# A hybrid encoder layer with 32 experts: the last two products trade places, the overflow count is read early, the final norm's row and the bias rows move

## The chip, the cores and the metric

The kernel runs on 1 core of one Trainium2 chip. The metric is the device time of one execution in microseconds; smaller is better. A core has a TensorE (PE in the rows; its weight loads are PEld), a VectorE (DVE), a ScalarE (ACT), a GpSimd (POOL), and a SyncE (SP) that here does nothing but issue transfers and read a few registers. Sixteen DMA engines carry the transfers.

## The reference

One encoder layer over 256 tokens of width 1024, and a final norm. A mixer (gated delta rule beside a short convolution) is followed by a mixture of experts, and the change lies in the second of these alone.

```python
def moe_ffn(h, router_w, router_b, w1, b1, w2, b2):
    logits = (hf @ router_w + router_b).astype(jnp.float32)
    top_val, top_idx = lax.top_k(logits, TOP_K)          # 4 of 32 experts for each token
    gates = jax.nn.softmax(top_val, axis=-1)
    ...
    def expert_block(args):
        gu = x_blk @ w1[e] + b1[e]                       # 1024 -> 2048
        gate, up = jnp.split(gu, 2, axis=-1)
        gate = jnp.minimum(gate, SWIGLU_LIMIT)
        up = jnp.clip(up, -SWIGLU_LIMIT, SWIGLU_LIMIT)
        act = gate * jax.nn.sigmoid(SWIGLU_ALPHA * gate) * (up + 1.0)
        return act @ w2[e] + b2[e]                       # 1024 -> 1024
    ...
x = x + gt_f * moe_ffn(...)
return rmsnorm(x, final_norm_w)
```

All 32 experts are used, in float32: 8 MB of `w1` and 4 MB of `w2` each.

## The kernel before, in words

After the mixer, the 32 experts are worked in 16 pairs, p = 0 to 15; two pairs form one of eight groups q (`NQ`). Pairs 0 and 1 are the experts 0 to 3; from group 1 on the experts are sorted by their load, and SP reads their numbers into registers (`pidx_i`, L1576) to form the addresses.

**First product, w1(p)** (`w1_pair`, L1372). Eight steps k. Each loads two tiles of 1 MB, one for each expert (`w1_load`), and makes 16 matmuls into four PSUM banks `pss[0..3]`: for each bank c, four matmuls j side by side on 32 columns of the array each (L1380). The fourth step calls `mid()`. After the last step four small matmuls add the bias (`w1_bias`, L119). Then `swiglu` (L1359 to L1363) makes half 0 from the banks 0 and 2, half 1 from 1 and 3: on DVE a minimum g, a clip u and two products, on ACT a tanh. `to_ff` transposes both halves on PE (L1397, eight transposes) and copies them to `aT` on ACT (L1398).

**Second product, w2(p)** (`w2_pair`, L1417). Four steps c, each again two tiles of 1 MB (L1426) and 16 matmuls (L1432). Then `combine`: DVE scales by the residual gate (L1414), PE spreads the rows back to the tokens (L1405), DVE adds to `x1` (L1407).

**Order of the pairs.** w1(0), then for p = 1 to 15: w1(p), w2(p-1), `to_ff` of p. So the swiglu of a pair has the second product of the pair before it to hide behind. Pair 15 ends with `w2_cols`: its second product in three parts of 512, 256 and 256 columns (`PARTS`; loads L1449, matmuls L1456), each followed by `combine` and by its share of the final norm (`finish_part`, L1558, L1549).

**Buffers and queues.** All weight tiles come from a ring of 18 places (`w_half`, L954): a load waits until the matmuls that read the tile 18 places before it are done. All loads go out on SP, in order, and at most eight are under way at once. A library places the instructions of each engine: it may move those that are not pinned (`pin`) past others, so the order of an engine is not always that of the program text.

**Three small things.** `final_row`, called from `mid()` of pair 2, loads the final norm's weights as two rows of 512 (L1563) and spreads them over the partitions by a matmul (L1566). Its tile `row` shares the buffer `u` of the swiglu, of which there is one. `route_rest` makes, beside the sorted order, the integer `nov`, the number of tokens that find no place in their expert's block. Behind the last `combine` every engine reads `nov` into a register (L1602) and branches (L1603): the overflow code is skipped when it is zero, as it is here.

Of the kernel before, what the change touches and what calls it, by code (L numbers as in the profile page):

```python
# [10 lines left out]
FT = mybir.dt.float32  # L11
# [3 lines left out]
AF = mybir.ActivationFunctionType  # L15
# [6 lines left out]
KT = D // 128  # L22
H = 8
NE = 32
# [4 lines left out]
NQ = 8  # L29
# [24 lines left out]
def encoder_block(ctx, tc, x, c, ada_w, ada_b, norm1_w, w_in, conv_qkv_w, a_log, dt_bias, onorm_w,  # L54
                  w_up_a, conv_sc_w, w_out_sc, w_o, norm2_w, router_w, router_b, moe_w1, moe_b1,
                  moe_w2, moe_b2, final_norm_w, out, dbg=None):
    nc = tc.nc
    V, A, G, PE = nc.vector, nc.scalar, nc.gpsimd, nc.tensor
# [22 lines left out]
    half_m = consts.tile([128, 1], FT, name="half_m")  # L81
    G.memset(half_m, -0.5)

    pin = tc.keep_in_program_order
# [25 lines left out]
    def misc(n=512):  # L110
        return pm.tile([128, n], FT, name="misc", tag="pt", bufs=2)

    def acc():
        return pm.tile([128, 512], FT, name="acc", tag=next(accs), bufs=3)

    def w1_bias(pa, bsel, b1c, pss, parts=(0, 1, 2, 3), first=False, pinned=False):
        for c in parts:
            b = 32 * c
            i = PE.matmul(pss[c], bsel[b:b + 32, pa * 128:(pa + 1) * 128], b1c[b:b + 32], start=first, stop=not first,  # L119
                          tile_position=(b, 0), skip_group_check=True)  # L120
            if pinned:
                tc.keep_in_program_order(i)
# [9 lines left out]
    with ExitStack() as mix:  # L132
# [26 lines left out]
        warm = consts.tile([128, 1], FT, name="warm")  # L159
# [6 lines left out]
        for i, b in enumerate(eb):  # L166
# [10 lines left out]
                        None, op0=OP.mult)  # L177
# [173 lines left out]
        for j in range(4):  # L351
# [12 lines left out]
            w = ep.tile([128, KT, 256], FT, name="raw", tag="raw", bufs=6) \  # L364
# [13 lines left out]
            for kk in range(2):  # L378
                k = 2 * j + kk
# [594 lines left out]
        def w1_load(p, k, regs):  # L974
            w = pre.pop((p, k), []) if p < 2 else []
            for m in range(len(w), 2):
                w.append(quarters(w1_tile(p, k, m, regs)[0]))
            return w
# [190 lines left out]
        pss0, bias_parts = [], []  # L1169
# [26 lines left out]
    work = ctx.enter_context(tc.tile_pool(name="work", bufs=1))  # L1196
# [30 lines left out]
    b1c, bsel0 = rbox[3:5]  # L1227
# [5 lines left out]
    nov = moe.tile([1, NE + 1], I32, name="nov")  # L1233
# [11 lines left out]
    def members(q):  # L1245
        off = 0
        for m, g in enumerate(GROUPS[min(q, 1)]):
            yield 4 * q + m, off, 32 * g
            off += 32 * g

    def bias_rows(q):
        bsel = work.tile([128, QS], FT, name="bsel", tag="bsel", bufs=1)
        for cpos, off, n in members(q):
            V.tensor_copy(bsel[:, off:off + n], perm[:, cpos:cpos + 1].to_broadcast([128, n]))
        return bsel
# [25 lines left out]
    for k, m, ts in ((KT - 2, 0, [fw, spare("pg"), spare("pgT")]), (KT - 2, 1, [spare("aT", 1024), spare("aT", 1024)]),  # L1281
                     (KT - 1, 0, [spare("g"), spare("g"), spare("u"), spare("th")]),
                     (KT - 1, 1, [spare("ysb"), spare("ysb"), e4])):
        c, qs = 0, []
# [40 lines left out]
    def xq_tile():  # L1325
        return work.tile([128, KT, QS], FT, name="XT", tag="XT", bufs=1)
# [11 lines left out]
    def gates_of(q):  # L1338
        pg = work.tile([128, 2, QS], FT, name="pg", tag="pg", bufs=1)
        for t in range(2):  # L1340
            for cpos, off, n in members(q):
                V.tensor_scalar(pg[:, t, off:off + n], iota[:, 0:n], rks[:, 0, t, cpos:cpos + 1],
                                rks[:, 1, t, cpos:cpos + 1], op0=OP.is_equal, op1=OP.mult)
        p = misc()
        for pa in range(2):
            for t in range(2):
                PE.transpose(p[:, (pa * 2 + t) * 128:(pa * 2 + t + 1) * 128], pg[:, t, pa * 128:(pa + 1) * 128], ident)
        gt = work.tile([128, 2, 2, 128], FT, name="pgT", tag="pgT", bufs=1)
        A.copy(gt, p.rearrange("p (a t n) -> p a t n", a=2, t=2))
        return gt  # L1350

    def owners(q):
        return [m for m, g in enumerate(GROUPS[min(q, 1)]) for _ in range(g)]
# [18 lines left out]
    def w1_pair(p, xq, bsel, pss, regs, mid):  # L1372
        q, pa = divmod(p, 2)
        own = owners(q)[4 * pa:4 * pa + 4]
        first = p == 0
        for k in range(KT):
            w = w1_load(p, k, regs)
            for c in range(4):
                for j in range(4):
                    PE.matmul(pss[c][j * 32:(j + 1) * 32], xq[:, k, (4 * pa + j) * 32:(4 * pa + j + 1) * 32],  # L1380
                              w[own[j] % 2][c], start=k == 0 and not first, stop=k == KT - 1 and first,
                              tile_position=(0, 32 * j), skip_group_check=True)
            if first and k < KT - 2:
                gather_part(P0, xq, (k + 2,))
            if k == 3:
                mid()
        if not first:
            w1_bias(pa, bsel, b1c, pss)
        return [swiglu(128, pss[half], pss[2 + half]) for half in range(2)]

    def to_ff(gs):
        aT = work.tile([128, KT, 128], FT, name="aT", tag="aT", bufs=2)
        for half in range(2):
            ps = misc()
            for i in range(4):
                c0 = 256 * (i // 2) + i % 2
                PE.transpose(ps[:, i * 128:(i + 1) * 128], gs[half][:, c0:c0 + 255:2], ident)  # L1397
            A.activation(aT[:, 4 * half:4 * half + 4], ps.rearrange("p (f n) -> p f n", f=4), AF.Copy, scale=0.5)  # L1398
        return aT
# [9 lines left out]
    def w2_rows(p, m, regs):  # L1409
        return moe_w2[0, 2 * p + m:2 * p + m + 1] if p < 2 else moe_w2[0, ds(regs[2 * (p % 2) + m], 1)]  # L1410
# [7 lines left out]
    def w2_pair(p, aT, gt, regs):  # L1418
        q, pa = divmod(p, 2)
        own = owners(q)[4 * pa:4 * pa + 4]  # L1420
        ys = [acc() for _ in range(2)]
        for c in range(4):
            w = []
            for m in range(2):
                t = w_half()
                nc.sync.dma_start(t, w2_rows(p, m, regs)[:, 256 * c:256 * c + 256].rearrange("e (p i) n -> p (e i n)", i=2))  # L1426
                w.append(t.rearrange("p (i n) -> p i n", i=2))
            for i in range(2):
                f = 2 * c + i
                for h in range(2):  # L1430
                    for j in range(4):
                        PE.matmul(ys[h][j * 32:(j + 1) * 32], aT[:, f, j * 32:(j + 1) * 32],  # L1432
                                  w[own[j] % 2][:, i, 512 * h:512 * h + 512], start=f == 0, stop=f == KT - 1,
                                  tile_position=(0, 32 * j), skip_group_check=True)
        for h in range(2):
            combine([gt[:, pa]], [scaled(ys[h], 512 * h, 512)], 512 * h, 512)
# [98 lines left out]
    xq = xq_tile()  # L1535
# [22 lines left out]
            V.tensor_tensor(xf[:, t, cs], x1[:, t, cs], fw[:, cs], op=OP.mult)  # L1558

    def final_row():  # L1560
        for h in range(2):
            row = work.tile([128, 512], FT, name="row", tag="u", bufs=1)[0:1]
            nc.sync.dma_start(row, bass.AP(tensor=final_norm_w.tensor, offset=final_norm_w.offset + 512 * h,  # L1563
                                           ap=[[D, 1], [1, 512]]))
            p = misc()
            PE.matmul(p, one_f[0:1], row, start=True, stop=True)  # L1566
            A.copy(fw[:, 512 * h:512 * h + 512], p)


    aTs, gts, regs, bsel = {}, {}, [None] * NQ, bsel0  # L1570
    nxt = []
    NP = 2 * NQ
    for p in range(NP):
        q, pa = divmod(p, 2)
        if pa == 0 and q:
            _, regs[q] = nc.values_load_multi_w_load_instructions(  # L1576
                pidx_i[0:1, 4 * q:4 * q + 4], engines=[mybir.EngineType.SP], min_val=0, max_val=NE - 1)

        def mid():
            if p == 2:  # L1580
                final_row()
            if pa == 1:
                gts[q] = gates_of(q)
                if q + 1 < NQ:
                    nxt.append(slots_of(q + 1))

        gs = w1_pair(p, xq, bsel, [acc() for _ in range(4)] if p else pss0, regs[q], mid)
        if p == 0:
            route_rest()
        if pa == 1 and q + 1 < NQ:  # L1590
            xq = gather(nxt.pop())
            bsel = bias_rows(q + 1)
        if p:
            w2_pair(p - 1, aTs.pop(p - 1), gts[(p - 1) // 2], regs[(p - 1) // 2])
        aTs[p] = to_ff(gs)
    xf = work.tile([128, KT, QS], FT, name="XT", tag="XT", bufs=1).rearrange("p (t a) b -> p t (a b)", t=2)
    for i, (c0, n) in enumerate(PARTS):
        w2_cols(NP - 1, c0, n, aTs[NP - 1], gts[NQ - 1], regs[NQ - 1])
        if i < len(PARTS) - 1:
            finish_part(xf, i)  # L1600

    n_over = nc.values_load(nov[0:1, NE:NE + 1], min_val=0, max_val=8 * NE)  # L1602
    with tc.If(n_over > 0):  # L1603
        ov = work.tile([128, KT, 128], FT, name="over", tag="aT", bufs=2).rearrange("p b n -> p (b n)")
        V.tensor_tensor(rks[:, 0], rks[:, 0], capr[:, None, :].to_broadcast([128, 2, NE]), op=OP.subtract)
        with tc.For_i(0, NE, 1) as cp:
# [6 lines left out]
            with tc.For_i(0, nb, 1) as b:  # L1613
# [7 lines left out]
                p = misc()  # L1621
# [10 lines left out]
                p = misc()  # L1632
# [4 lines left out]
                for half in range(2):  # L1637
                    pss = [acc() for _ in range(2)]
                    for gu in range(2):
                        bs = slice(32 * (2 * gu + half), 32 * (2 * gu + half) + 32)  # L1640
                        PE.matmul(pss[gu][0:32], ohe[bs].to_broadcast([NE, 32]), b1c[bs],
                                  start=True, stop=False, tile_position=(bs.start, 0), skip_group_check=True)
# [67 lines left out]
```

## Time and profile before

| what | value |
|---|---|
| median of 3 runs | 1381.16 us (1380.38 to 1382.26) |
| the profiled execution: its own time | 1382.46 us |
| the profiled execution: span of the core | 1380.7 us |
| busy share of the span: PE, DVE, ACT, POOL | 97%, 37%, 20%, 11% |
| bytes read from HBM | 486.82 MB |
| mean granted TensorE clock | 0.991 of full speed |

The profiled execution took 1.3 us longer than the median. Its span runs from the first to the last instruction. A busy PE is not PE at its peak, since matmuls are pipelined and their ends are modelled.

### The profile page before, as it was taken

Reading aid. Unit: us, or ns where it says so; the run is one execution under the profiler, and the core shown is the slowest. Engines: PE = TensorE matmul, PEld = TensorE weight load, DVE = VectorE, ACT = ScalarE, POOL = GpSimd, SP = SyncE. Lnnn points to the kernel's source line nnn. Section 1 sums busy time; section 2 is a strip of 40 time slices with the busy share of each in tenths; the row PEclk is TensorE's granted clock in tenths of the full one; section 3 lists DMA queues with packets and bytes.
Section 4 is the critical chain, followed back from the end, with each engine's and each line's share of the span. In section 5 each row is a group of like instructions: output and inputs, shape, how many; then the busy total and the mean of one; then the engine's idle time right before and its main releaser. Section 6 shows DMA issues by size and latency. Waiting matters only on the chain.

```text
span 1380.7 us, 24523 instructions
## 1 busy us (share of the span) xinstructions
PE 1338.9 (97%) x10250; PEld 688.6 (50%) x10251; DVE 512.0 (37%) x1017; ACT 280.0 (20%) x544; POOL 150.9 (11%) x125
## 2 busy tenths in 40 slices
PE   6999998899999999999999999999999999999996
PEld 4898887899996333233333333333333333333322
DVE  3377879965773332113113022120311212031123
ACT  3465562554642010000000000000000000010001
POOL 4555685000100000000000000000000000000000
PEclk9999999999999999999999999999999999999998
DMA  9978977247698999999999999999999999999995
GB/s 336 291 250 267 303 234 245 76 147 251 227 363 301 385 381 421 410 420 420 420 422 420 421 421 420 421 420 422 420 421 420 421 422 420 421 420 421 421 382 169
DMA packets 134708, 492.68 MB, mean 357 GB/s; under 512 B 11070, under 2 KB 68799, under 8 KB 86977
## 3 DMA queue, kind: packets, MB, share of 16 engines
q1 hardware_dynamic: 130548, 486.08, 89.6%
q10 hardware_dynamic: 4045, 4.98, 1.1%
q8 instruction: 82, 1.34, 0.4%
q14 instruction: 33, 0.27, 0.1%
HBM read 486.82 MB, written 4.21 MB: 356 GB/s over the span
## 4 chain that ended last, share of the span: by engine, by line
issue 65%; POOLq 0%; ACT 0%
POOLq L1705 0%; ACT XT L1678 0%
## 5 line engine op out<-in xcount | busy, mean ns | idle before, releaser
L1380 PE MATMUL acc<-wst,XT 128*32 128x512 f32 x4088 | 543.7, 595 | 0.0
L1380 PEld LDWEIGHTS acc<-wst,XT 128*32 128x32 f32 x4088 | 154.5, 110 | 350.0 <-issue 332.9
L1432 PE MATMUL acc<-wst,aT 128*32 128x512 f32 x1920 | 234.9, 595 | 2.0 <-DMA wst<-in_moe_w_dram 2.0
L1359 DVE TENSOR_SCALAR g<-acc 128x512 f32<-128x512 f32 x32 | 20.7, 687 | 387.6 <-PE acc L119 383.5
L313 PE MATMUL mm<-hh,wl 128*128 128x256 f32 (+1 forms) x520 | 149.3, 287 | 5.0 <-DVE wl L263 3.6
L311 PE MATMUL mm<-hh,wh 128*128 128x256 f32 (+1 forms) x520 | 151.3, 291 | 1.2 <-DVE cacc L556 1.2
L312 PE MATMUL mm<-hl,wh 128*128 128x256 f32 (+1 forms) x520 | 149.5, 288 | 0.0
L1432 PEld LDWEIGHTS acc<-wst,aT 128*32 128x32 f32 x1920 | 68.4, 109 | 145.6 <-issue 131.2
L88 POOL TENSOR_TENSOR rs<-ss,half_m 128x2 f32<-128x2 f32 x3 | 2.1, 703 | 1008.5 <-DVE ss L1672 943.5
L262 ACT CAST wh<-raw 128x1024 fp32r<-128x1024 f32 (+1 forms) x89 | 91.7, 1038 | 94.7 <-PE mm L312 55.0
L311 PEld LDWEIGHTS mm<-hh,wh 128*128 128x128 f32 (+1 forms) x520 | 100.2, 193 | 12.5 <-issue 8.1
L313 PEld LDWEIGHTS mm<-hh,wl 128*128 128x128 f32 (+1 forms) x520 | 100.1, 193 | 7.2 <-DVE wl L263 3.8
L312 PEld LDWEIGHTS mm<-hl,wh 128*128 128x128 f32 (+1 forms) x520 | 100.2, 193 | 0.9 <-issue 0.8
L1398 ACT ACTIVATE aT<-misc 128x512 f32<-128x512 f32 x32 | 17.6, 595 | 387.9 <-PE misc L1397 387.9
L263 POOL TENSOR_TENSOR wl<-raw,wh 128x1024 fp32r<-128x1024 f32 x36 | 87.7, 2444 | 71.6 <-ACT wh L262 65.7
L1407 DVE TENSOR_TENSOR x<-x,misc 128x512 f32<-128x512 f32 (+1 forms) x66 | 44.3, 671 | 80.1 <-PE misc L1405 80.1
L263 DVE TENSOR_TENSOR wl<-raw,wh 128x1024 fp32r<-128x1024 f32 (+1 forms) x53 | 63.8, 1209 | 24.7 <-ACT wh L262 24.3
L1360 ACT ACTIVATE th<-g 128x512 f32<-128x512 f32 x32 | 20.2, 630 | 254.6 <-DVE g L1359 210.2
L1414 DVE TENSOR_TENSOR ysb<-acc,gtf 128x512 f32<-128x512 f32 (+1 forms) x33 | 22.3, 675 | 125.6 <-PE acc L1432 113.5
L1405 PE MATMUL misc<-ysb,pgT 128*128 128x512 f32 (+1 forms) x132 | 63.9, 606 | 2.0 <-DVE ysb L1414 1.9
L1323 ACT ACTIVATE XT<-misc,mod,afc 128x256 f32<-128x256 f32 x32 | 17.3, 561 | 167.9 <-PE acc L1380 126.1
L556 DVE SCALAR_TENSOR_TENSOR cacc<-mm,col,cacc 128x254 f32<-128x254 f32 (+1 forms) x96 | 46.1, 480 | 9.0 <-ACT cacc L553 6.9
(388 smaller groups left out, 1396.9 us busy)
## 6 DMA issues: line engine op xcount, KB each, us to landing
wst<-in_moe_w_dram SPq DMA_DIRECT2D x372, 1024.0 KB, 19.8
raw<-in_w_in_dram SPq DMA_DIRECT2D x36, 1024.0 KB, 7.4
raw<-in_ada_w_dram SPq DMA_DIRECT2D x24, 1024.0 KB, 8.5
wst<-in_moe_w_dram SPq DMA_DIRECT2D x24, 256.0 KB, 7.6
wst<-in_moe_w_dram SPq DMA_DIRECT2D x11, 512.0 KB, 15.1
raw<-in_w_out_sc_dram SPq DMA_DIRECT2D x4, 1024.0 KB
raw<-in_w_up_a_dram SPq DMA_DIRECT2D x4, 1024.0 KB, 5.2
raw<-in_w_o_dram SPq DMA_DIRECT2D x4, 1024.0 KB, 13.3
```

Source lines behind the costliest of these rows:

```text
L262: a = A.copy(wh, src)
L263: b = (V if job.lo == "v" else G).tensor_tensor(wl, src, wh.bitcast(FT), op=OP.subtract)
L311: PE.matmul(ps, wh[:, k, :], ah[:, k, :], start=k == 0, stop=False, skip_group_check=True)
L312: PE.matmul(ps, wh[:, k, :], al[:, k, :], start=False, stop=False, skip_group_check=True)
L313: PE.matmul(ps, wl[:, k, :], ah[:, k, :], start=False, stop=k == KT - 1, skip_group_check=True)
L556: V.scalar_tensor_tensor(a[:, o0:o1], p[:, s0:s1], cw(j), a[:, o0:o1], op0=OP.mult, op1=OP.add)
L1359: V.tensor_scalar(g[:n], g_ps[:n], 7.0, None, op0=OP.min)
L1380: PE.matmul(pss[c][j * 32:(j + 1) * 32], xq[:, k, (4 * pa + j) * 32:(4 * pa + j + 1) * 32], w[own[j] % 2][c], start=k == 0 and not first, ...
L1405: PE.matmul(p[:, 0:n], gt[pa][:, t], ysb[pa], start=pa == 0, stop=pa == len(ysb) - 1)
L1407: V.tensor_tensor(xv, xv, p[:, 0:n], op=OP.add)
L1414: V.tensor_tensor(y, ps[:, 0:n], gtf_box[0][:, c0:c0 + n], op=OP.mult)
L1432: PE.matmul(ys[h][j * 32:(j + 1) * 32], aT[:, f, j * 32:(j + 1) * 32], w[own[j] % 2][:, i, 512 * h:512 * h + 512], start=f == 0, stop=f == ...
```

## The change

The order of the last two products is turned round: w2(14) now stands before w1(15), and the transposes and the three parts of pair 15 follow w1(15) directly. For all pairs but pair 0 the four bias matmuls stand first in w1(p) and not last (pair 0 has had it so). The overflow count is read behind w1(4) in the program text, with a pinned instruction on DVE, ACT and POOL behind it. The two rows of the final norm use the buffers `pg` and `P`, one each, and not `u` twice. The gates of group 7 are made ahead of w2(14). The arithmetic is the same but for the order of the bias in the sums.

```diff
     def w1_pair(p, xq, bsel, pss, regs, mid):
         q, pa = divmod(p, 2)
         own = owners(q)[4 * pa:4 * pa + 4]
-        first = p == 0
+        if p:
+            w1_bias(pa, bsel, b1c, pss, first=True)
         for k in range(KT):
             w = w1_load(p, k, regs)
             for c in range(4):
                 for j in range(4):
                     PE.matmul(pss[c][j * 32:(j + 1) * 32], xq[:, k, (4 * pa + j) * 32:(4 * pa + j + 1) * 32],
-                              w[own[j] % 2][c], start=k == 0 and not first, stop=k == KT - 1 and first,
+                              w[own[j] % 2][c], start=False, stop=k == KT - 1,
                               tile_position=(0, 32 * j), skip_group_check=True)
...
-        if not first:
-            w1_bias(pa, bsel, b1c, pss)
         return [swiglu(128, pss[half], pss[2 + half]) for half in range(2)]
...
     def final_row():
-        for h in range(2):
-            row = work.tile([128, 512], FT, name="row", tag="u", bufs=1)[0:1]
+        for h, tag in enumerate(("pg", "P")):
+            row = work.tile([128, 512], FT, name="row", tag=tag, bufs=1)[0:1]
...
-        if p:
-            w2_pair(p - 1, aTs.pop(p - 1), gts[(p - 1) // 2], regs[(p - 1) // 2])
-        aTs[p] = to_ff(gs)
...
+    for p in range(NP - 1):
+        first_product(p)
+        if p == 4:
+            n_over = nc.values_load(nov[0:1, NE:NE + 1], min_val=0, max_val=8 * NE)
+            pin(V.memset(warm, 0.0))
+            pin(A.activation(warm, warm, AF.Tanh))
+            pin(G.memset(half_m, -0.5))
+        if p:
+            second_product(p - 1)
+        aTs[p] = to_ff(gs.pop(p))
+    gts[NQ - 1] = gates_of(NQ - 1)
+    second_product(NP - 2)
+    first_product(NP - 1)
+    aTs[NP - 1] = to_ff(gs.pop(NP - 1))
...
-    n_over = nc.values_load(nov[0:1, NE:NE + 1], min_val=0, max_val=8 * NE)
     with tc.If(n_over > 0):
```

How the instructions of an engine stand before and after the change, at three places. Line numbers shift by -1 or +1 in between.

TensorE at the end, before: L1380 and L119 are w1(15) with its bias, L1432 and L1405 are w2(14) with its `combine`, L1397 the transposes of pair 15, L1456 its first part.

```order
L1380 MATMUL acc<-wst,XT 32x512 x96
L119 MATMUL acc<-b1c,bsel 128x512 x4
L1432 MATMUL acc<-wst,aT 32x512 x64
L1405 MATMUL misc<-ysb,pgT 128x512 x4
L1397 MATMUL misc<-ident,g 128x128 x8
L1456 MATMUL acc<-wst,aT 32x512 x32
```

The same stretch of TensorE now (L1431 is w2(14), L1404 its `combine`, L1381 is w1(15), L1396 the transposes, L1455 the first part):

```order
L1431 MATMUL acc<-wst,aT 32x512 x42
L1404 MATMUL misc<-ysb,pgT 128x512 x2
L1381 MATMUL acc<-wst,XT 32x512 x8
L1404 MATMUL misc<-ysb,pgT 128x512 x2
L1381 MATMUL acc<-wst,XT 32x512 x120
L1396 MATMUL misc<-ident,g 128x128 x8
L1455 MATMUL acc<-wst,aT 32x512 x32
```

Nothing stands between the last matmul of w1(15) and the transposes of its swiglu any more, and all eight transposes stand ahead of the first part.

TensorE around w1(2), before: L1566 are the two matmuls of the final norm's rows, L119 the bias of pair 2, L1432 is w2(1).

```order
L1380 MATMUL acc<-wst,XT 32x512 x15
L1566 MATMUL misc<-row,one_f 128x512
L1380 MATMUL acc<-wst,XT 32x512 x64
L119 MATMUL acc<-b1c,bsel 128x512 x4
L1432 MATMUL acc<-wst,aT 32x512 x13
L1566 MATMUL misc<-row,one_f 128x512
L1432 MATMUL acc<-wst,aT 32x512 x51
```

The same stretch now, from the end of w2(0) (L1431 x3) to the start of w1(3):

```order
L1431 MATMUL acc<-wst,aT 32x512 x3
L119 MATMUL acc<-b1c,bsel 128x512 x4
L1381 MATMUL acc<-wst,XT 32x512 x3
...
L1381 MATMUL acc<-wst,XT 32x512 x23
L1565 MATMUL misc<-row,one_f 128x512 x2
L1381 MATMUL acc<-wst,XT 32x512 x64
L1431 MATMUL acc<-wst,aT 32x512 x64
L119 MATMUL acc<-b1c,bsel 128x512 x4
```

The bias of pair 2 and both row matmuls now stand ahead of the last four steps of w1(2) (the 64); before, one row matmul did. In the same way two of the four bias matmuls of pair 1 moved to a place ahead of w1(0), behind the routing, and two to a place ahead of w1(1).

VectorE at the end, before:

```order
L1414 TENSOR_TENSOR ysb<-acc,gtf 128x256
L1407 TENSOR_TENSOR x_4177<-x_4177,misc 128x256 x2
L1602 TENSOR_LOAD nov
L1603 COMPARE_AND_BRANCH
L1605 TENSOR_TENSOR rks<-rks,capr 128x64
```

And now, first in `route_rest`, where `nov` is made, then at the end:

```order
L1515 CAST nov<-nof 1x33
L1603 TENSOR_LOAD nov
L1604 MEMSET warm 128x1
L1524 TENSOR_TENSOR b2c<-b2c,gtf 32x256 x4
...
L1413 TENSOR_TENSOR ysb<-acc,gtf 128x256
L1406 TENSOR_TENSOR x_4177<-x_4177,misc 128x256 x2
L1620 COMPARE_AND_BRANCH
L1622 TENSOR_TENSOR rks<-rks,capr 128x64
```

The register load has left the end of DVE; the branch stays. On PE the load still stands at the end; on SP and POOL it stood early before as well.

## Rows read from the trace of the kernel before

**Rows 1.** Windows: stretch, busy us of five engines, granted clock, DMA share, GB/s.

```profile
484.00:494.00 10.00, 10.00 (x92) 2.96 (x88) 2.76 (x7) 0.45 (x1) 0.00 (x0) 1.00 0.87 319
514.00:518.00 4.00, 4.00 (x32) 1.48 (x22) 1.09 (x2) 0.00 (x0) 0.00 (x0) 1.00 0.83 312
557.00:567.00 10.00, 10.00 (x96) 2.91 (x88) 0.00 (x0) 0.00 (x0) 0.00 (x0) 1.00 1.01 380
567.00:1320.00 753.00, 752.42 (x5496) 251.68 (x5494) 152.92 (x318) 47.86 (x84) 0.00 (x0) 1.00 1.01 421
1320.00:1363.00 43.00, 40.63 (x316) 13.35 (x311) 12.75 (x19) 3.90 (x8) 0.00 (x0) 1.00 0.92 336
1363.00:1371.00 8.00, 6.34 (x84) 3.34 (x73) 3.21 (x8) 1.02 (x4) 0.00 (x0) 1.00 0.00 1
```

**Rows 2.** Waits of SP's queue, whole run: us in total, times, longest.

```profile
SPq L968 <- DMA wst<-in_moe_w_dram: 364.4, 189, 3.5
...
SPq L1563 <- DVE g L1362: 9.2, 1, 9.2
```

**Rows 3.** Timeline of SP around the first row: start us, us.

```profile
513.85 0.30 SPq L1563 DMA_DIRECT2D row<-in_final_norm_w_dram  x1
514.38 11.48 SPq L968 DMA_DIRECT2D wst<-in_moe_w_dram  x7
```

**Rows 4.** Timeline of PE, 506 to 567 us: bias, w2(0), row, w1(2).

```profile
506.27 1.14 PE L119 MATMUL acc<-b1c,tri_ul 32*128 32x512 f32 x8
...
512.95 2.76 PE L1432 MATMUL acc<-wst,aT 128*32 128x512 f32 x18
...
551.38 1.12 PE L1566 MATMUL misc<-row,one_f 1*128 1x512 f32 x2
552.43 13.94 PE L1380 MATMUL acc<-wst,XT 128*32 128x512 f32 x128
```

**Rows 5.** Timeline of PE at the end, in brackets the idle time before.

```profile
1341.07 3.62 PE L1432 MATMUL acc<-wst,aT 128*32 128x512 f32 x20 [0.58 <-DMA wst<-in_moe_w_dram]
1344.71 3.86 PE L1405 MATMUL misc<-ysb,pgT 128*128 128x512 f32 x8
1348.49 1.60 PE L1397 MATMUL misc<-ident,g 128*128 128x128 f32 x8
1350.03 7.07 PE L1456 MATMUL acc<-wst,aT 128*32 128x512 f32 x64
...
1365.10 3.66 PE L1456 MATMUL acc<-wst,aT 128*32 128x256 f32 x64
```

**Rows 6.** Timeline of DVE, swiglu of pair 15: first clip, last product.

```profile
1326.71 0.68 DVE L1361 TENSOR_SCALAR u<-acc 128x512 f32<-128x512 f32 x1
...
1330.40 0.69 DVE L1363 SCALAR_TENSOR_TENSOR g<-th,g 128x512 f32<-128x512 f32 x1
```

**Rows 7.** Timeline of DVE at the end.

```profile
1370.07 0.85 DVE L1407 TENSOR_TENSOR x<-x,misc 128x256 f32<-128x256 f32 x2 [0.79 <-PE misc L1405]
1372.48 0.43 DVE L1558 TENSOR_TENSOR XT<-x,fw 128x256 f32<-128x256 f32 x1 [1.56 <-DVEq L1603]
```

**Rows 8.** Loads of the overflow count by engine: duration ns, start us.

```profile
L1602 POOLq TENSOR_LOAD <-nov x1: 499/499/499, 483.0 to 483.0; - x1
...
L1602 DVEq TENSOR_LOAD <-nov x1: 542/542/542, 1371.1 to 1371.1; - x1
```

**Rows 9.** Timeline of PE, two idle times in the mixer.

```profile
222.32 1.06 PE L908 MATMUL pt<-raw,crep 128*32 128x512 f32 x8 [1.66 <-DMA raw<-in_ada_w_dram]
...
231.48 0.84 PE L916 MATMUL dd<-ident,adas 128*128 128x128 f32 x4 [2.50 <-DVE adas L913]
```

**Rows 10.** Windows around two falls of the granted clock, columns as in rows 1.

```profile
231.80:235.20 3.40, 3.40 (x19) 3.40 (x17) 3.26 (x6) 1.99 (x2) 1.26 (x1) 0.50 0.74 242
...
426.40:429.80 3.40, 3.37 (x16) 1.57 (x15) 1.79 (x15) 1.42 (x6) 1.57 (x13) 1.00 0.51 154
429.80:436.60 6.80, 6.25 (x20) 3.84 (x24) 5.72 (x22) 3.36 (x9) 0.61 (x7) 0.50 0.92 293
```

More of the change, by code (lines that the diff above doesn't have):

```diff
@@ L1380, in w1_pair @@
                     PE.matmul(pss[c][j * 32:(j + 1) * 32], xq[:, k, (4 * pa + j) * 32:(4 * pa + j + 1) * 32],
-                              w[own[j] % 2][c], start=k == 0 and not first, stop=k == KT - 1 and first,
+                              w[own[j] % 2][c], start=False, stop=k == KT - 1,
                               tile_position=(0, 32 * j), skip_group_check=True)
-            if first and k < KT - 2:
+            if p == 0 and k < KT - 2:
                 gather_part(P0, xq, (k + 2,))
@@ L1567, in final_row, with first_product @@
             A.copy(fw[:, 512 * h:512 * h + 512], p)
-    aTs, gts, regs, bsel = {}, {}, [None] * NQ, bsel0
-    nxt = []
+    aTs, gts, regs, gs, bsel = {}, {}, [None] * NQ, {}, bsel0
     NP = 2 * NQ
-    for p in range(NP):
+    def first_product(p):
+        nonlocal xq, bsel
         q, pa = divmod(p, 2)
+        nxt = []
         if pa == 0 and q:
@@ L1582, in mid, with second_product @@
             if pa == 1:
-                gts[q] = gates_of(q)
+                if q + 1 < NQ:
+                    gts[q] = gates_of(q)
                 if q + 1 < NQ:
                     nxt.append(slots_of(q + 1))
-        gs = w1_pair(p, xq, bsel, [acc() for _ in range(4)] if p else pss0, regs[q], mid)
+        gs[p] = w1_pair(p, xq, bsel, [acc() for _ in range(4)] if p else pss0, regs[q], mid)
         if p == 0:
             route_rest()
-        if pa == 1 and q + 1 < NQ:
+        if nxt:
             xq = gather(nxt.pop())
             bsel = bias_rows(q + 1)
-        if p:
-            w2_pair(p - 1, aTs.pop(p - 1), gts[(p - 1) // 2], regs[(p - 1) // 2])
-        aTs[p] = to_ff(gs)
+    def second_product(p):
+        w2_pair(p, aTs.pop(p), gts[p // 2], regs[p // 2])
+    for p in range(NP - 1):
[5 more added lines that the diff above has]
+            pin(G.memset(half_m, -0.5))
+        if p:
+            second_product(p - 1)
[4 more added lines that the diff above has]
+    aTs[NP - 1] = to_ff(gs.pop(NP - 1))
     xf = work.tile([128, KT, QS], FT, name="XT", tag="XT", bufs=1).rearrange("p (t a) b -> p t (a b)", t=2)
```

## Prediction

> **What bounds the kernel now.** I first read the windows from the end of the mixer on. From 567 to 1320 us the sixteen DMA engines are never idle (share 1.01) and carry 421 GB/s [rows 1]; the engines' busy shares say nothing there, since what ends last is a transfer. SP's own waits agree: in nearly every issue of a weight tile it waits for one that went out eight places earlier, 364.4 us in 189 waits at L968 alone, never more than 3.5 us [rows 2]. PE follows the transfers. So in the middle only a gap in the stream can be won, and work on PE, DVE or ACT costs nothing as long as buffers come free in time.
>
> The stream is not full everywhere. Before 567 us there are three weak stretches: 10 us at 319 GB/s from 484, 4 us at 312 from 514, 10 us at 380 from 557 [rows 1]. Held against 421 they are worth 2.4, 1.0 and 1.0 us; that is all the front can give.
>
> At the end the bound changes. The smaller loads of `w2_cols` come at 336 GB/s, and after 1363 us nothing is loaded any more [rows 1]. PE, however, starts its last part at 1365.10 [rows 5], two microseconds behind the transfers. From the last step of w2(14) on, the chain is PE's: last step 1341.07 to 1344.69, `combine` to 1348.5, transposes, first part from 1350.03 [rows 5]. Behind PE stands DVE: the last sum of `x1` ends at 1370.92, and its next piece of work starts 1.56 us later, behind the branch [rows 7]. These two places decide what the change is worth.
>
> **The change, part by part.** The sum is made against the profiled execution's own 1382.46 us, which lies 1.30 us above the median of 1381.16; I take the differences over to the median.
>
> *The order of the last products.* Now 5.34 us lie between the last matmul of w2(14) (1341.07 + 3.62 = 1344.69) and the first part of pair 15 (1350.03): `combine` and eight transposes. After the change the same bytes stand in the queue at that place, so w1(15) makes its last step at the same time; call its end T. Then follows the swiglu, which before was hidden behind w2(14). From its first clip to its last product it takes 1330.40 + 0.69 - 1326.71 = 4.38 us [rows 6]. With the bias in front, the banks finish one after the other, a quarter of 3.62 us apart, and the first clip reads bank 2, so it can start about 0.8 us ahead of T (0.9, less a hand-over of 0.1). The last product ends at T + 3.6, the transposes of half 1, half of 1.60 us, at T + 4.4, and the first part starts. That is 0.9 us earlier than now. Bounds: 0, if the clip only starts behind T and the transposes are no shorter, and 1.3, if the second four transposes take 0.4 us. The `combine` of pair 14 goes into w1(15), whose loads come slower than PE works them. The transfers allow it: the last part would start near 1364.2, still after 1363.
>
> *The clock.* In those 4.4 us PE does nothing but four short transposes in the middle. The trace has such places: after 2.50 us idle at 231.48 the granted clock was 0.50 from 231.8 to 235.2, the lower of its two levels (1.2 instead of 2.4 GHz), while 1.66 us at 222.32 left it at full speed [rows 9, 10]. So I expect a stretch of 3.4 us at the lower level. If all of it falls on the first part, the work in it takes double, and 1.7 us are lost; if it begins before the first part does, less. I take 1.3. Bounds: 0, and 3.4 for 6.8 us, as from 429.8 on [rows 10]. The transposes hardly help: the 3.4 us before 429.8 show PE busy for 3.37 us, with transposes and other short matmuls, and the clock fell all the same [rows 10]. The Trainium skill ("TensorE: Matmul & The Clock Gate", Part 4: PE-mode transpose) says that transposes don't count as work of the engine in the same way. By that rule the two halves of the gap are one gap, and the term stays 1.3; if they counted, it would be 0. The rows agree in direction, but none shows transposes alone.
>
> *The overflow count.* DVE's load took 0.54 us behind the last sum [rows 8], and waiting and the branch make up the rest of the 1.56 us [rows 7]. Without the load the branch can be taken while the sum still runs. I take 1.0 us won; bounds 0.5 (the load alone) and 1.5 (the gap vanishes). The load now stands in `route_rest` on DVE and ACT, 0.5 us each. Behind it wait the products for the second bias; this lies under w1(1). POOL's load already stood there and started at 483.0 us, as soon as the count was there [rows 8]. If its cover were gone, it would cost its 0.5 us. PE's load stays at the end, and nobody waits for it.
>
> *The row's buffers.* SP waited 9.2 us for `u` before the first row [rows 2], until 513.85, with the weight load behind it at 514.38 [rows 3]. It looks like a gain of the 1.0 us missing from 514 to 518. But that load needs the place of a tile of w2(0), and its matmuls, 4 of the 9 (18 records) that start at 512.95 [rows 4], end near 514. Whoever takes the row's wait away finds this one. I take 0.1, bounds 0 and 1.0. The second row waits for the gather from `P`, which ends before the next weight load could go.
>
> *Bias first, rows together.* Four bias matmuls take 1.14 us, a row 1.12 [rows 4]. Two of pair 1's four moved into an idle time before the stream. So the last four steps of w1(2) (552.43 to 566.4) come 1.14 + 1.12 - 0.57 = 1.7 us later, and their tiles come free later, just where the stream is weak (557 to 567). Each load that finds no free place delays all behind it. With up to eight loads under way I take 0.3 lost; bounds 0 and 1.7. The order in which SP reads its registers ahead of group 1's loads changes a little; the hole of 2.4 us at 484 [rows 1] may shrink or stay. I take 0, bounds 0 and the 2.4 as a gain. In all later pairs the bias lies under the stream, as before.
>
> **Sum.** -0.9 + 1.3 - 1.0 - 0.1 + 0.3 = -0.4: own time 1382.1, and from the median 1380.8 us.
>
> **The rivals.**
> 1. *The clock holds.* The gap of 4.4 us holds two groups of transposes of 0.8, so some 2.8 us idle, or 1.4 each if they lie apart, which is shorter than the 1.66 us that did no harm [rows 9]. Then the 1.3 go: 1379.5. Against it stands the stretch before 429.8. Chance 0.22.
> 2. *The clock stays low twice as long* (slower). If the first part, begun at half speed, doesn't lift it at once, 6.8 us cost 3.4 instead of 1.3: 1382.9. It decides from 1.7 us of loss on, since the other terms sum to -1.7; a measurement would tell it from 4.4 us on. For it: after 429.8 PE was busy for 6.25 of 6.8 us and the clock stayed low. Against it: at 231.8 a full load lifted it after 3.4 us. Chance 0.10.
> 3. *The front gives its holes back.* If the row's 1.0 and the 2.4 us at 484 are both won and stay won up to the end: 1380.8 - 1.0 - 2.4 + 0.1 (the row's term, counted already) = 1377.5. Against it: both stretches are set by places in the ring, and those come free no earlier. Chance 0.10.
> 4. *It does nothing*: the swiglu chain is no shorter than `combine` and transposes, DVE's branch costs what the load hid, the clock holds: 1381.2. Chance 0.08.
>
> **How the numbers follow.** The forecast has 0.50. Its own range, with the clock's 1.3 kept and the other terms' distances to their bounds added as squares (the root of 0.4, 0.5, 0.9 and 0.3 squared is 1.1 below, of 0.9, 0.5, 0.1 and 1.4 squared 1.7 above), is 1379.7 to 1382.5. The range for 8 in 10 takes in rivals 1 and 4, and 2 up to its price, and stops short of 3: 1377.8 to 1383.0. What a measurement of this kernel can tell from no change is about 0.2%, 2.8 us, so faster means under 1378.4 and slower over 1383.9. Rival 3, with the lower part of rival 1, makes 0.24 faster; the upper part of rival 2, and a front that loses its 1.7 us as well, 0.08 slower; the rest, 0.68, is the same.
>
> **What would show it.** In the profile after: the first part of pair 15 starting about 4.4 us behind the last matmul of w1(15); a granted clock of 0.5 for 3.4 us around that start; no register load between DVE's last sum and its next piece, and a gap there of about 0.6 us in place of 1.56; from 514 to 518 us about the same 312 GB/s as now; from 557 to 567 us no more than 380. Wrong would be the forecast if the weights ended clearly before or after 1363 us, since the front then moved the stream; or if the first part started later than 1350, since the swiglu's chain then isn't shortened by the order of the banks.

## The result, and the profile after

The changed kernel is slower: 1403.92 us (5 runs, 1402.34 to 1404.99) against 1381.36 us, a ratio of 1.0164 (95% interval 1.0152 to 1.0176), or 22.6 us. The forecast was 1380.8 us in a range of 1377.8 to 1383.0.

The waits of SP's queue show first what became of the stream (line, what it waited for, us in total, times, longest us):

```profile
SPq L1425 <- PE acc L1381: 185.0, 63, 12.4
SPq L968 <- DMA wst<-in_moe_w_dram: 148.8, 90, 3.0
SPq L968 <- PE acc L1431: 135.8, 45, 10.9
SPq L968 <- PE acc L1381: 125.9, 92, 4.3
```

Now most of the waiting is for PE: a load finds its place in the ring still in use. Before, most loads waited for a transfer ahead of them, 364.4 us at L968 [rows 2], but not all. This line of before stands between those of rows 2:

```profile
SPq L968 <- PE acc L1380: 50.2, 30, 3.9
```

With 45.6 us of the same kind at L1426, and nearly all of both ahead of 900 us, it says that PE was behind the stream at first and worked this backlog off. Now it no longer does: PE has become the slower of the two. How much slower, two groupings of PE's instructions show. Each spans exactly two pairs in the middle, 512 matmul records of the first product and 256 of the second (a matmul shows as two records), from the start of w1(7) to that of w1(9) before, and from w1(9) to w1(11) now. These starts are the last row of each timeline here (start us, us), first before, then after:

```profile
808.67 3.63 PE L1380 MATMUL acc<-wst,XT 128*32 128x512 f32 x16
...
926.38 3.63 PE L1380 MATMUL acc<-wst,XT 128*32 128x512 f32 x16
```

```profile
943.25 2.33 PE L1381 MATMUL acc<-wst,XT 128*32 128x512 f32 x9
...
1065.53 2.77 PE L1381 MATMUL acc<-wst,XT 128*32 128x512 f32 x12
```

So two pairs took PE 117.7 us before, without a gap, and 122.3 now. The weights alone, 48 MB (48 x 1,048,576 bytes), would take 119.5 us at 421 GB/s [rows 1]. With the small transfers beside them the stream needs 120.8: in the run below with the bias in one piece from pair 2 on, where PE waits for weights in the middle, two pairs take that long, and 50.81 MB arrive in it at 421 GB/s. PE stood 3.1 us under this pace, and now stands 1.5 above. From the first matmul of w1(2) to that of w1(14), PE took 699.9 us before (529.0 to 1228.9) and 723.8 now (531.1 to 1254.9), where the stream at this pace needs 6 x 120.8 = 724.8. Before, PE gained 24.9 us on the stream over these twelve pairs; now it gains 1.0. The grouping by line for these two stretches (busy us, mean ns, idle before; times of lines that run into each other overlap), before:

```profile
L1380 PE MATMUL acc<-wst,XT 128*32 128x512 f32 x512 | 71.1, 595 | 0.0
L1432 PE MATMUL acc<-wst,aT 128*32 128x512 f32 x256 | 30.0, 594 | 0.0
...
L119 PE MATMUL acc<-b1c,bsel 32*128 32x512 f32 x16 | 2.3, 640 | 0.0
```

And after:

```profile
L1381 PE MATMUL acc<-wst,XT 128*32 128x512 f32 x512 | 71.1, 595 | 0.0
L1431 PE MATMUL acc<-wst,aT 128*32 128x512 f32 x256 | 33.2, 595 | 0.0
...
L119 PE MATMUL acc<-b1c,bsel 32*128 32x512 f32 x16 | 5.1, 640 | 0.0
L1315 PE MATMUL misc<-P,h2h 128*128 128x256 f32 x16 | 4.5, 315 | 0.7 <-ACT XT L1323 0.7
```

Counts and mean durations of the products and the bias are the same. What grew is the time in which they fill the engine: the bias by 2.8 us and the second product, w2, by 3.2. The gathers (L1315) now have 0.7 us of idle time ahead of them, at the place where the bias stood before. The lines also overlap more, so that of these 6.7 us 4.6 are left in the time of two pairs. PE's timeline in the middle of w2(9), after, says why:

```profile
1046.94 1.68 PE L119 MATMUL acc<-b1c,bsel 32*128 32x512 f32 x6
1048.55 3.63 PE L1431 MATMUL acc<-wst,aT 128*32 128x512 f32 x24
1052.10 1.12 PE L119 MATMUL acc<-b1c,bsel 32*128 32x512 f32 x2
```

The bias of the next pair no longer stands behind the first product in one piece (before: four matmuls, eight records, 1.14 us at 850.55). The scheduler has put it into w2, in two pieces. One bias matmul alone, two records, takes 1.12 us: as long as all four side by side. The Trainium skill ("TensorE: Matmul & The Clock Gate", Why this matters for your kernels) says that matmuls of 32 rows on different row groups run at the same time, and that a single one takes no less than a full one; the trace agrees, 1.14 against 1.12 us, and a single matmul of 128 rows in w2 took 1.05 (at 996.35). And where the bias cuts into the four column groups of w2, fewer of them run side by side: 24 records took 3.63 us at 1048.55, where in the kernel before 32 took 3.66 (at 852.76).

At the end (PE's timeline after, in brackets idle time before, with what ended it):

```profile
1336.42 28.18 PE L1381 MATMUL acc<-wst,XT 128*32 128x512 f32 x240
1366.39 0.74 PE L1396 MATMUL misc<-ident,g 128*128 128x128 f32 x4 [1.79 <-DVE g L1363]
1368.56 1.12 PE L1396 MATMUL misc<-ident,g 128*128 128x128 f32 x4 [1.43 <-DVE g L1363]
1369.62 9.34 PE L1455 MATMUL acc<-wst,aT 128*32 128x512 f32 x64
1379.78 1.98 PE L1404 MATMUL misc<-ysb,pgT 128*128 128x512 f32 x4 [0.82 <-DVE ysb L1413]
```

w1(15) ends at 1336.42 + 28.18 = 1364.60 and never waits for a weight; before, each step of w2(14) but the first waited 0.4 to 0.6 us for one and the last ended at 1344.69 [rows 5]. From 1363 to 1371 us the windows show 40 GB/s: the weights of all three last parts are almost in, and PE has yet to start them. The stream ends little later than before; it is PE that is late. The windows on the clock there (columns as in rows 1):

```profile
1366.00:1369.40 3.40, 1.58 (x8) 1.28 (x8) 2.32 (x4) 1.23 (x2) 0.00 (x0) 0.71 0.00 0
1369.40:1371.00 1.60, 1.60 (x10) 0.40 (x12) 0.00 (x0) 0.60 (x1) 0.00 (x0) 0.50 0.00 0
1371.00:1372.80 1.80, 1.80 (x12) 0.40 (x8) 0.00 (x0) 0.00 (x0) 0.00 (x0) 0.50 0.00 0
1372.80:1376.00 3.20, 3.20 (x28) 0.88 (x24) 0.00 (x0) 0.00 (x0) 0.00 (x0) 0.77 0.00 0
```

By their means the clock was at the lower level for 2.0 us of the first window, all of the next two, and 1.5 us of the last: 6.8 us in all, from about 1367.4 to 1374.2.

The `combine` of the first part on PE and the end of DVE, before (rows that rows 5 and 7 leave out), then DVE after:

```profile
1357.91 1.98 PE L1405 MATMUL misc<-ysb,pgT 128*128 128x512 f32 x4 [0.81 <-DVE ysb L1414]
...
1374.68 0.88 DVE L1676 TENSOR_SCALAR XT<-XT,rs 128x512 f32<-128x512 f32 x2 [0.81 <-POOL rs L88]
```

```profile
1393.17 0.42 DVE L1557 TENSOR_TENSOR XT<-x,fw 128x256 f32<-128x256 f32 x1 [0.39 <-DVEq L1620]
...
1395.43 0.88 DVE L1693 TENSOR_SCALAR XT<-XT,rs 128x512 f32<-128x512 f32 x2 [0.88 <-POOL rs L88]
```

The 22.1 us between the spans (1402.8 less 1380.7) come together so: the last product ends 1364.60 - 1344.69 = 19.9 later; from there to the `combine` of the first part it takes 15.2 us (to 1379.78), not 13.2 (to 1357.91), 2.0 more; the gap on DVE is 0.39 and not 1.56, 1.2 less; and from DVE's last work to the end of the span it takes 6.5 us (1402.8 - 1396.31) and not 5.1 (1380.7 - 1375.56), 1.4 more.

The front (windows after, and two of before that rows 1 leave out):

```profile
470.00:484.00 14.00, 14.00 (x120) 6.45 (x119) 8.73 (x36) 2.12 (x5) 0.05 (x1) 1.00 0.72 284
484.00:494.00 10.00, 10.00 (x90) 3.02 (x92) 3.23 (x9) 0.68 (x2) 0.05 (x1) 1.00 1.00 394
514.00:518.00 4.00, 4.00 (x36) 1.28 (x36) 0.55 (x1) 0.56 (x1) 0.00 (x0) 1.00 0.90 322
518.00:557.00 39.00, 39.00 (x270) 12.30 (x270) 8.58 (x24) 3.50 (x6) 0.00 (x0) 1.00 0.97 396
557.00:567.00 10.00, 10.00 (x100) 3.01 (x95) 0.97 (x4) 0.00 (x0) 0.00 (x0) 1.00 0.95 360
```

```profile
470.00:484.00 14.00, 14.00 (x127) 6.02 (x130) 8.46 (x37) 1.98 (x5) 0.00 (x0) 1.00 0.83 335
518.00:557.00 39.00, 39.00 (x285) 12.41 (x288) 6.97 (x17) 2.91 (x5) 0.00 (x0) 1.00 1.01 421
```

The stretch from 484 us gained 10 x 75 / 421 = 1.8 us of the stream, those from 470, 518 and 557 lost 1.7, 2.3 and 0.5. From 557 us the low rate of before is no idle stretch: the engines' share is 1.01 at 380 GB/s [rows 1].

### The profile page after: what moved, and what is told of

It is laid out like the page before. It is cut to its first block, busy times and chain, and to the rows that moved or that the text cites. A ratio compares the mean times of both kernels' runs of the same rounds, so it can differ in the third digit from the quotient of the medians.

```text
span 1402.8 us, 24525 instructions
## 1 busy us (share of the span) xinstructions
PE 1358.1 (97%) x10250; PEld 692.8 (49%) x10251; DVE 513.4 (37%) x1018; ACT 279.4 (20%) x545; POOL 151.0 (11%) x126
## 5 line engine op out<-in xcount | busy, mean ns | idle before, releaser
L1381 PE MATMUL acc<-wst,XT 128*32 128x512 f32 x4088 | 543.4, 597 | 0.0
L1381 PEld LDWEIGHTS acc<-wst,XT 128*32 128x32 f32 x4088 | 153.8, 110 | 350.4 <-issue 341.0
L1431 PE MATMUL acc<-wst,aT 128*32 128x512 f32 x1920 | 244.7, 599 | 0.0
L1431 PEld LDWEIGHTS acc<-wst,aT 128*32 128x32 f32 x1920 | 68.4, 110 | 142.2 <-issue 136.0
L313 PEld LDWEIGHTS mm<-hh,wl 128*128 128x128 f32 (+1 forms) x520 | 99.9, 192 | 7.1 <-DVE wl L263 3.8
L1397 ACT ACTIVATE aT<-misc 128x512 f32<-128x512 f32 x32 | 17.9, 595 | 409.6 <-PE misc L1396 409.5
L1404 PE MATMUL misc<-ysb,pgT 128*128 128x512 f32 (+1 forms) x132 | 64.7, 608 | 2.0 <-DVE ysb L1413 1.9
L1323 ACT ACTIVATE XT<-misc,mod,afc 128x256 f32<-128x256 f32 x32 | 16.9, 563 | 172.4 <-PE acc L1381 120.8
```

The source lines that it names most:

```text
L313: PE.matmul(ps, wl[:, k, :], ah[:, k, :], start=False, stop=k == KT - 1, skip_group_check=True)
L1404: PE.matmul(p[:, 0:n], gt[pa][:, t], ysb[pa], start=pa == 0, stop=pa == len(ysb) - 1)
```

## The experiments

Theory A: the cut bias lifts PE's time for two pairs over the stream's pace, PE falls behind pair by pair, and the end waits for PE. The expectations take the stream's pace as 119.2 us, not the 120.8 above. Each ratio is to the kernel before on the same chip. First the parts of the change, alone and undone.

**The bias last again,** the rest of the change kept:

```diff
-        if p:
-            w1_bias(pa, bsel, b1c, pss, first=True)
...
+        if not first:
+            w1_bias(pa, bsel, b1c, pss)
         return [swiglu(128, pss[half], pss[2 + half]) for half in range(2)]
```

> The changed kernel with the four bias matmuls of pairs 1 to 15 last again; the other three parts stay. Theory A (in the changed kernel the early bias is cut in pieces among the matmuls of the second product, and PE then needs 122.2 us for two pairs where the weight stream needs 119.2, so PE itself is late at the end): two pairs take PE 117.7 us again, the last step of w1(15) ends within 6 us of the landing of its weights instead of 22 us behind, and the time is 1382 (1380 to 1384), about 1 us over before for the low clock in the tail. Rival B (the turned order of the last two products holds PE up): it stays at 1400 or more. Rival C (the 2.9 us that the stream loses before 570 us come from the rows and grow): 1384 to 1387.

1386.68 us, 1.0034 (1.0020 to 1.0048). From w1(7) to w1(9), 807.6 to 925.3 us, PE's second product and bias are back at the figures of before:

```profile
L1432 PE MATMUL acc<-wst,aT 128*32 128x512 f32 x256 | 30.0, 594 | 0.0
...
L119 PE MATMUL acc<-b1c,bsel 32*128 32x512 f32 x16 | 2.3, 640 | 0.0
```

Rival B, that the turned order holds PE up, is out. What stays is more than A expected, some 5 us over before, and the time lies in the range of rival C, the rows. The three other parts alone decide that: they follow, and come to 1.0030, 1.0000 and 1.0009, in sum 1.0039 against the 1.0034 here. With the 1.0119 of the bias alone the four parts come to 1.0158 of the 1.0164.

**The bias first alone,** in the kernel before (the diff above the other way round):

> The kernel before with the bias first alone. Theory A: PE needs over 121 us for two pairs, falls behind the stream from about 700 us on, and the time is 1398 to 1404. Rival B: 1381 to 1384, since the last products stand as before. Rival C: 1381 to 1383, since the rows stand as before.

1398.16 us, 1.0119 (1.0101 to 1.0136): 16.4 of the 22.6 us. w2 and bias fill 33.2 and 5.1 us for two pairs, as in the changed kernel. Rivals B and C are out as main causes.

**The turned order alone:**

```diff
-    for p in range(NP):
+    for p in range(NP - 1):
...
+    second_product(NP - 2)
+    first_product(NP - 1)
+    aTs[NP - 1] = to_ff(gs.pop(NP - 1))
```

> The kernel before with the turned order of the last two products alone. Theory A: stream and PE as before up to w1(15); then 5.0 us from its last matmul to the first part in place of 5.3, and the first part takes 9.3 us in place of 7.1 at the low clock: 1383 (1382 to 1385). Rival B: 1398 or more.

1385.55 us, 1.0030 (1.0016 to 1.0044), above A's range. With the bias behind w1(15), PE's timeline at the end is

```profile
1341.56 1.14 PE L119 MATMUL acc<-b1c,bsel 32*128 32x512 f32 x8
1346.19 1.13 PE L1397 MATMUL misc<-ident,g 128*128 128x128 f32 x4 [3.48 <-DVE g L1363]
...
1349.42 8.02 PE L1456 MATMUL acc<-wst,aT 128*32 128x512 f32 x64
1358.27 1.98 PE L1405 MATMUL misc<-ysb,pgT 128*128 128x512 f32 x4 [0.82 <-DVE ysb L1414]
```

The swiglu now waits for the bias too: the first part starts 6.7 us behind the last bias (1342.70), not 5.0, and takes 8.0 us, not 9.3. From the last bias to the `combine` it takes 15.6 us, against 13.2 before. That is 2.4 of the 4.1 us that the ratio gives; where the rest goes the profiled execution, faster than its median (1382.63), does not show.

**The early load of the count alone:**

```diff
+        if p == 4:
+            n_over = nc.values_load(nov[0:1, NE:NE + 1], min_val=0, max_val=8 * NE)
+            pin(V.memset(warm, 0.0))
...
-    n_over = nc.values_load(nov[0:1, NE:NE + 1], min_val=0, max_val=8 * NE)
```

> The kernel before with the early load of the overflow count alone. Every theory: the gap between DVE's last sum and its next work shrinks from 1.56 to 0.39 us as in the changed kernel, nothing else moves: 1380.2 (1379.5 to 1381). If something else on that chain ends last behind it, 1381.3.

1382.51 us, 1.0000 (0.9989 to 1.0011). DVE's gap is 0.39 us, but nothing arrives at the end. Windows of the output's transfers, here and (second fence) in the kernel before:

```profile
1373.50:1376.50 3.00, 0.00 (x0) 0.00 (x0) 0.00 (x0) 0.29 (x1) 0.00 (x0) 0.50 0.91 329
1376.50:1379.00 2.50, 0.00 (x0) 0.00 (x0) 0.00 (x0) 0.00 (x0) 0.00 (x0) 0.50 0.08 31
```

```profile
1375.70:1378.70 3.00, 0.00 (x0) 0.00 (x0) 0.00 (x0) 0.31 (x1) 0.00 (x0) 0.50 0.86 320
1378.70:1379.80 1.10, 0.00 (x0) 0.00 (x0) 0.00 (x0) 0.00 (x0) 0.00 (x0) 0.50 0.22 82
```

Here one engine's worth of traffic (31 GB/s, a share of 0.08) trails for 2.5 us. The queues in the half microsecond from 1374.0, with the early count, hold the output and an instruction load together (packets, MB, share):

```profile
q1 hardware_dynamic: 90, 0.18, 97.0%
q8 instruction: 1, 0.02, 21.6%
```

Before, such a load stands ahead of the output's first packet (alone from 1374.7 to 1375.2, 14.8%). Where PE's own load of the count stands at the end, as the change leaves it, it starts 4.7 to 5.2 us behind that load in all twelve traces that show both (before: 1375.1 and 1370.0; here: 1374.1 and 1368.9). The output follows DVE, has become earlier by DVE's gain, and meets it. In the four runs with DVE's load early and PE's at the end (this, the changed kernel, the bias last again, and the last below) the end behind DVE's last work takes 5.9 to 7.2 us. In the run with the two products pinned, PE's load too has moved early (674.5 us): DVE's gap is 0.39, the instruction load starts at 1378.1, ahead of the output (1379.5), and that end takes 5.1 us, as before. So the 1.2 us seem to arrive once PE's load is early as well; no run moved that alone.

**The rows alone** (`("pg", "P")` in place of `u`):

> The kernel before with the two rows of the final norm in the buffers of the changed kernel, alone. Theory A: 514 to 518 us gains little, the loads there wait for the place of a tile next; 1381.6 (1380.5 to 1383). Rival C (the rows cost the stream some 3 us before 570 us): 1384 or more.

1383.04 us, 1.0009 (1.0001 to 1.0018): about 1.2 us lost, nothing won. The 3 us of rival C are out, a third of them is not.

**The cut bias kept, the two products pinned,** in the changed kernel:

```diff
-                    PE.matmul(pss[c][j * 32:(j + 1) * 32], xq[
+                    pin(PE.matmul(pss[c][j * 32:(j + 1) * 32], xq[
...
-                        PE.matmul(ys[h][j * 32:(j + 1) * 32],
+                        pin(PE.matmul(ys[h][j * 32:(j + 1) * 32],
```

> The changed kernel, with the matmuls of the first and the second product kept in the order of the program text (for each weight tile pair, four columns of the array side by side); the early bias is still cut in pieces. Theory A: the steps that now run on two columns at a time and take 7.3 us instead of 3.5 are gone, two pairs cost PE under 112 us, the stream sets the pace again, the last step of w1(15) ends within 6 us of the landing of its weights: 1384 (1380 to 1388), with the loss in the tail as in the kernel with the turned order alone. Rival D (the early bias hurts through its waits for the banks or through later released tiles, not through PE's time): 1399 or more.

1383.36 us, 1.0016 (1.0000 to 1.0032). The same two pairs on PE (810.2 to 928.7 us):

```profile
L1381 PE MATMUL acc<-wst,XT 128*32 128x512 f32 x512 | 61.7, 594 | 4.0 <-DMA wst<-in_moe_w_dram 4.0
...
L119 PE MATMUL acc<-b1c,bsel 32*128 32x512 f32 x16 | 5.6, 640 | 1.0 <-DVE u L1361 1.0
```

The bias is as cut as in the changed kernel, 5.6 us. But the first product takes 61.7 us in place of 71.1, w2 31.4 in place of 33.2, PE waits 4.0 us for weights again, and 20 of the 22.6 us are gone. Rival D, harm by the bias's own waits, is out; what counts is PE's sum against the stream.

**The bias twice,** in odd pairs and in all, one more line behind the bias: `if p % 2: w1_bias(pa, bsel, b1c, pss)`, and the same without the condition.

> The kernel before, with the bias added twice in every odd pair (the output differs by that): four more matmuls in one piece, 1.1 us for two pairs. Theory A (PE has 119.2 - 117.7 = 1.5 us spare in two pairs): 118.8 us, still under the stream; the last weights are met with no backlog and the time is that of before, 1382 (1381 to 1384). Rival E (each microsecond of PE costs one): 8 x 1.1 = 9 us more, 1391.

1382.00 us, 1.0003 (0.9994 to 1.0013), as A has it. From w1(5) to w1(9) (689.5 to 926.4 us) two pairs take 118.4 us in the mean, under the stream's pace.

> The kernel before, with the bias added twice in all pairs from 1 on (the output differs by that): 2.2 us more for two pairs. Theory A: 119.9 us against the stream's 119.2; the backlog no longer drains, PE enters w1(15) some 8 to 15 us behind and the time is 1390 (1386 to 1396). Rival E: 15 x 1.1 = 17 us more, 1399. If PE had room for it: 1382.

1381.39 us, 0.9995 (0.9986 to 1.0004): A's number is missed by 9 us. Part of the miss is A's pace: its 119.9 us for two pairs lie over 119.2, but under 120.8, and then nothing had to be lost. And PE did not take 119.9. The two pairs from w1(5) to w1(7) (690.2 to 802.2 us):

```profile
L1380 PE MATMUL acc<-wst,XT 128*32 128x512 f32 x512 | 61.8, 594 | 0.0
...
L119 PE MATMUL acc<-b1c,bsel 32*128 32x512 f32 x32 | 4.0, 613 | 0.0
```

The bias took its 1.7 us more, but the scheduler laid the first product out anew and it fills 61.8 us, 9.3 less than before. PE's sum fell, to 112.0 us, and 1.8 of these are waits for weights. So this run did not add what it was to add; it agrees with A only in that PE under the pace costs nothing. How much more work PE could take was not measured with the rest held still.

**The bias first in one piece,** pinned (`first=True, pinned=True`), and then the same from pair 2 on (`pinned=p > 1`):

> The kernel before with the bias first, but pinned: its four matmuls stand together directly ahead of the pair's first step. Theory A (the cost lies in the cut pieces, not in the place): PE stays under 119 us for two pairs, 1382 (1378 to 1385). Rival F (a bias that opens the banks holds the first step up wherever it stands): 1396 or more.

1398.39 us, 1.0119 (1.0104 to 1.0134), a miss for A, in the range of rival F. One window of it:

```profile
466.50:490.50 24.00, 18.79 (x88) 12.54 (x80) 14.96 (x54) 4.25 (x8) 0.00 (x0) 0.59 0.23 97
```

Pair 1's pinned bias waits behind the routing, its first product behind it, and the queue runs dry: 24 x (421 - 97) / 421 = 18.5 us.

> The kernel before with the bias first, its four matmuls pinned in one piece from pair 2 on, pair 1 left to the scheduler. Theory A with the reading of the run before (the pinned bias of pair 1 alone emptied the queue from 470 to 490 us, and from 560 us on PE kept up with the stream): no hole there, PE under the stream's pace, 1381 (1378 to 1385). Rival F (a bias in front costs its 16 us in the stream wherever it stands): 1396 or more.

1384.26 us, 1.0011 (1.0002 to 1.0021). Without that hole the loss is gone but for 1.5 us. PE waits for weights in the middle again, here from 810.0 to 930.8 us:

```profile
L1431 PE MATMUL acc<-wst,aT 128*32 128x512 f32 x256 | 34.9, 596 | 2.1 <-DMA wst<-in_moe_w_dram 2.1
```

Rival F is out: a bias in front costs little, if it waits for nothing late. How much of this is the one piece is not shown by itself, since the scheduler laid the products out anew here too: the first fills 66.5 us, not 71.1, and w2 34.9.

**A better end:** the transposes of pair 15 ahead of w2(14), in the kernel before.

```diff
+        if p == NP - 1:
+            aTs[p] = to_ff(gs)
         if p:
             w2_pair(p - 1, aTs.pop(p - 1), gts[(p - 1) // 2], regs[(p - 1) // 2])
-        aTs[p] = to_ff(gs)
+        if p < NP - 1:
+            aTs[p] = to_ff(gs)
```

> The kernel before with the transposes of pair 15 ahead of w2(14) in the program text; they then stand behind its first step, where PE waits for weights anyway. Theory A (behind w2(14) the chain is PE's alone): the first part starts at about 1348.5 in place of 1350.0, 1380 (1379 to 1381.5). If the last loads or the swiglu of pair 15 hold the first part instead: 1381.6.

1380.41 us, 0.9989 (0.9979 to 0.9998). PE at the end:

```profile
1330.90 0.72 PE L1397 MATMUL misc<-ident,g 128*128 128x128 f32 x4 [1.46 <-DVE g L1363]
1331.55 11.65 PE L1432 MATMUL acc<-wst,aT 128*32 128x512 f32 x96
...
1347.01 7.07 PE L1456 MATMUL acc<-wst,aT 128*32 128x512 f32 x64
```

The first part starts 3.8 us behind w2(14), not 5.3, the transposes being hidden, and the clock holds.

> The same with the early load of the overflow count. If its 1.2 us at DVE reach the end: 1379 (1378 to 1380.5), below both kernels; if the output's transfers give them back, as in the kernel with the early load alone: 1380.

1380.66 us, 0.9993 (0.9982 to 1.0005): the early count adds nothing, as alone, with PE's load of it at the end (1367.1 us).

## Why the prediction was wrong, point by point

**What bounds the kernel: the step that failed.** "PE follows the transfers. So in the middle only a gap in the stream can be won, and work on PE, DVE or ACT costs nothing as long as buffers come free in time." A transfer did set the pace, but the conclusion does not follow. The prediction read SP's waits as waits for transfers "in nearly every issue"; at L968 these are 189 waits among 252 issues, and more than 95 us of waits for PE stand beside them. It set PE's busy 752.42 of 753 us [rows 1] aside. PE was behind the stream for most of that stretch, waited for no weight from 567 to 1200 us, and was at work on its backlog. Of w1(15) the prediction says that its "loads come slower than PE works them", which holds for a single step in full: 3.5 us [rows 4] against 5.0 for two loads. But the steps that run on half the columns (16 records in 3.63 us at 808.67), the `combine`, the gathers and the transposes fill most of the rest. For two pairs PE had 3.1 us to spare in 120.8. Nothing was worked out for PE's sum over a pair, and no rival had PE as the bound.

**"In all later pairs the bias lies under the stream, as before": a cost of 0 that was 16 us.** Its rows were eight records in one piece, 1.14 us [rows 4], and the orders quoted showed it whole for pairs 2 and 3, with pair 1 alone split. That a piece of one costs as much as four, and what a piece does to the matmuls that it cuts, was not priced; no order of the later pairs is shown. 5.1 us of bias and 33.2 of w2 in place of 2.3 and 30.0, with 0.7 of idle time, took PE over the pace, and the bias alone gives 1.0119.

**The order of the last products: mis-sized.** -0.9 was forecast; from the last matmul to the first part it is 5.0 us, not 4.4, against 5.3 before. The first clip started 0.5 us ahead of the last matmul's end (1364.13), not 0.8, and the second four transposes took 1.12 us at half clock, not 0.8.

**The clock: right in kind, mis-sized.** It fell, to 0.50 before the first part, but for 6.8 us and not for 3.4: the length of rival 2. The first part took 9.34 in place of 7.07 us: 2.3 lost, 1.3 forecast, 3.4 the price of rival 2, since some of the 6.8 us lay ahead of it. Rival 1 fell. By the rule of the Trainium skill that the prediction cites ("TensorE: Matmul & The Clock Gate", Part 4: PE-mode transpose) the two idle times of 1.79 and 1.43 us would be one gap. The trace agrees but does not prove it: no row here shows 1.79 us by itself, and with the turned order alone the clock fell inside the idle time of 3.48 us, ahead of any transpose (0.77 from 1342.6 to 1346.2). With its cost the turned order loses where it should have won: 2.0 us in the tail, and alone 1.0030.

**The count: right at DVE, wrong at the end.** 1.2 us won at the gap against 1.0 forecast; the kernel with this alone shows 1.0000. The time behind DVE's last work was taken as fixed, and grew. "PE's load stays at the end, and nobody waits for it" is the step that failed here, as far as the traces tell: an instruction load follows PE's load, and now falls among the output.

**Row and front.** The row's 0.1 gain was right in size for 514 to 518 us (322 for 312 GB/s), but the whole part alone gives 1.0009, a loss. At the front 2.7 us are lost on balance where 0.3 was forecast and 1.7 the bound; the place named, 557 to 567, lost least of it. In a kernel that ends on PE this no longer adds up with the rest.

Open are some 2 of the 4.1 us that the turned order costs alone, and what the instruction load behind PE's load of the count brings.

## What to carry to other kernels

Work out each engine's time for one turn of the loop, and set it beside the transfers' time, all transfers counted. An engine that is busy 99.9% of a stretch may be working off a backlog; here it had 3.1 us to spare in 120.8, though its single steps look short. One matmul cut out of a small group that shares the array cost as much as the whole group; when a scheduler may move it, read the order in every turn, or pin the group, but never behind something late.

## What the runs showed of the hardware

Four bias matmuls of 32 rows side by side took 1.14 us, one alone 1.12. In twelve runs an instruction load of 0.02 MB started 4.7 to 5.2 us behind PE's load of a register; with one among the 1 MB of output, the output's last 2.5 us went at 31 GB/s in one run, and the end took 5.9 to 7.2 us in four runs against 5.0 to 5.5 in the ten others. And four transposes between two idle times of 1.79 and 1.43 us did not keep the granted clock from falling to 0.50, where it stayed for 6.8 us.
